# A two-block transformer kernel: square sums on TensorE, order of a turn, one more raw buffer, work behind the last turn

## The chip, the core and the metric

The kernel runs on one core of one Trainium2 chip. The metric is the device time of one execution in microseconds (us), the median of three runs. TensorE (PE in the rows; its weight loads are PEld) multiplies matrices, VectorE (DVE) and ScalarE (ACT) work element by element, GpSimd (POOL) does a few small things, and SyncE (SP) issues nearly all transfers (DMAs) from memory. Each engine executes its own instructions strictly in the order of the program; a wait of one instruction holds up all behind it on that engine.

## The reference, cut to what matters

Two transformer blocks follow each other over 256 tokens of width 2048. The change touches the first stage of the first block's first layer only, which computes this, for the tokens `x` and for a context `ctx` of 256 tokens:

```python
def _rmsnorm(x, w):
    xf = x.astype(jnp.float32)
    y = xf * lax.rsqrt(jnp.mean(xf * xf, axis=-1, keepdims=True) + EPS)
    return (y * w.astype(jnp.float32)).astype(x.dtype)
...
    shift, scale, gate = jnp.split(jax.nn.silu(c) @ w_mod + b_mod, 3, axis=-1)
    hx = _rmsnorm(x, norm_w) * (1 + scale[:, None]) + shift[:, None]
    a_h, a_b, a_c, a_z, q, k, v, r_z = _split_in(hx @ w_in)
```

So before the first large product `hx @ w_in` can begin, the mean square of each token is wanted, and shift and scale, which are products of one vector with two thirds of the 2048 x 6144 matrix `w_mod`.

## The kernel before, in words

All data is float32. The features lie on the 128 partitions: x and ctx are 16 tiles of 128 features x 256 tokens each (`qT`, `kT`, `v` and `big1` hold them at first, 512 KB per transfer). A main weight is split into a rounded part `whi` (ScalarE) and a rest `wlo` (VectorE), and each product is made of three multiplications on TensorE; all of them have line L370.

The first stage runs in eight turns j = 0 to 7 (`mod0_cols`), one for every 256 of the 2048 features. A turn reads eight blocks of `w_mod` of 512 KB in four steps g = 0 to 3 of two blocks each, and TensorE multiplies each step's blocks in eight instructions (L490) into one side bank of PSUM. After g = 3 ScalarE copies that bank to `macc0` (L494), TensorE transposes it (L502), VectorE adds the parts up and adds the bias (`mod0_turn`: mcol, L473, L510), and `make_hx` builds two tiles of hx as `a` tiles (VectorE L526, ScalarE L527, VectorE L528). These two tiles are then multiplied by their rows of the k columns and half of the q columns of `w_in` (512 KB and 256 KB per turn): 36 multiplications in six pieces of six, which the next turn weaves between its four steps: two pieces behind g = 0, one behind g = 1, two behind g = 2, one behind g = 3 (turn 1 has none behind g = 0). The other 256 q columns follow behind the stage, again in eight units of two tiles each.

Ahead of the turns, `squares` takes the squares of x and ctx on ScalarE (eight instructions, L436), sums them over the tiles on VectorE (L439, L441), and in turn 0, behind g = 1, TensorE sums over the partitions (`tok_sums`, L232). VectorE and GpSimd take the root (L218), and `bcast_rows` spreads the result over the partitions with TensorE (L243), behind g = 2.

The blocks land in raw buffers: of the two blocks of a step the first takes the pool `wraw` (4 buffers, which the `w_in` blocks of the turn use too), the second the pool `wst` (3 buffers). SyncE issues in program order, and an issue waits until the buffer's last reader is through. TensorE's order is the order of the code; the scheduler orders the other engines, with priorities (`hot` puts work forward). Beside the later units a background queue `modq` sums the remaining columns of `w_mod` on VectorE (L458, L461), from its own raw blocks, also in `wraw`.

Of the kernel before, what the change touches and what calls it, by code (L numbers as in the profile page):

```python
# [13 lines left out]
AF = mybir.ActivationFunctionType  # L14
# [5 lines left out]
P = 128  # L20
# [142 lines left out]
def kernel(ctx: ExitStack, tc: tile.TileContext, x, cx, vec, w_mod, w_in, ret_decay_f, ret_decay_b,  # L163
# [7 lines left out]
    def mk(pool, shape, tag, dt=F32, bufs=None):  # L171
        uid[0] += 1
        return pool.tile(shape, dt, tag=tag, name=f"{tag}_{uid[0]}", bufs=bufs)
# [234 lines left out]
    xr = [None] * KT  # L408
    cr_ = [None] * KT
    rb = [None, None]  # L410
    xin = []
    for s, src in enumerate((x, cx)):
        for a in range(2):
# [17 lines left out]

    def squares(s):

        for g in range(4):
            sq = mk(ap_, [P, 1024], f"a{14 + g % 2}")
            nc.scalar.activation(out=sq, in_=xin[2 * s + g // 2][:, 4 * (g % 2):4 * (g % 2) + 4, :]  # L436
                                 .rearrange("p k t -> p (k t)"), func=AF.Square)
            acc = mk(tb, [P, L], "tmp") if g else sqa[s]
            nc.vector.tensor_reduce(out=acc, in_=sq.rearrange("p (k t) -> p t k", k=4), axis=AX.X, op=ALU.add)  # L439
            if g:  # L440
                nc.vector.tensor_tensor(out=sqa[s], in0=sqa[s], in1=acc, op=ALU.add)  # L441


    modc = [[smalls[f"mod{l}{v}"] for v in range(2)] for l in range(2)]
# [34 lines left out]
    def mod0_cols(j, weave):  # L479


        pr = side_ps()
        for g in range(4):
            raws = []
            for a in range(2):
                raws.append(mk(wst if a else wraw, [P, 2, 512], "raw"))
                nc.sync.dma_start(out=raws[a], in_=w_mod[j, 2 * g + a])
            for q in range(4):
                k = 4 * g + q
                nc.tensor.matmul(pr[32 * q:32 * q + 32, :], lhsT=s2w[:, 2 * k:2 * k + 32], rhs=raws[q // 2][:, q % 2, :],  # L490
                                 start=g == 0, stop=g == 3, tile_position=(0, 32 * q))
            if g == 3:
                row = mk(t1, [P, 512], "macc0")
                nc.scalar.copy(out=row, in_=pr)  # L494
                rows[j] = row
            weave(j, g)

# [161 lines left out]
    def layer(l):  # L659
# [30 lines left out]
        def qkv(g):  # L690
            nonlocal at
            if l == 0 and g == 0:
# [1 line left out]
                b = Block(wl, [(col("k", 0), 512), (col("q", 0), 256)], mov, T, "fm", KT)  # L694
                b.ps = [[main_ps() for _ in range(4)], [main_ps(), side_ps()]]
                line = []
                rinv = []

                def more(n):
                    for _ in range(n if line else 0):  # L700
# [3 lines left out]
                            line.pop(0)  # L704

                def weave(j, g):
                    if j == 0:
                        if g == 1:
                            for s in range(2):
                                rinv.append(rsq(mean_eps(tok_sums([sqa[s]]), 2, D), 2, f"rq{s}"))  # L710
                        if g == 2:
                            for s in range(2):
                                rb[s] = bcast_rows(rinv[s], 2, f"rb{s}")
                    else:
                        more((2, 1, 2, 1)[g] if j > 1 else (0, 1, 2, 1)[g])
                    if g == 3:
                        mod0_turn(j)
                        for k in (2 * j, 2 * j + 1):
                            make_hx(l, k)
                        line.append([b.steps([2 * j, 2 * j + 1], True), 6])  # L720
                        next(line[-1][0])
                        if j == 5:
                            nc.sync.dma_start(out=cr, in_=kcr)

                for j in range(KT // 2):
                    mod0_cols(j, weave)
                while line:
                    more(1)
                kT, qT = mk(t1, [P, 4, 512], "kT"), mk(t1, [P, 4, T], "qT")
# [6 lines left out]
                pumps.append(dmaq)  # L736
                pri[0] = PRI
                layer_tables(l)
                evac(qT, Block(wl, [(col("q", 0) + 256, 256)], mov, T, "fm", KT).run(ks)[0], 2, 1.0, T)
                rope(qT)  # L740
                ps = run("v", g, 512, "tm")
                v = mk(t1, [P, 4, 512], "v")
# [566 lines left out]
```

## Time and profile before

| | |
|---|---|
| median of 3 runs | 2839.34 us (2837.23 to 2842.5) |
| the profiled execution, its own time | 2839.79 us |
| its span, first to last instruction | 2838.1 us |
| PE busy | 2795.9 us, 99% of the span |
| DVE, ACT, POOL busy | 1777.6, 1224.9, 85.5 us |
| mean DMA rate | 184 GB/s |
| mean granted TensorE clock | 0.997 |

In the rows further below, engines stand in the order PE, PEld, DVE, ACT, POOL where they have no name. The busy share of PE counts matmuls whose ends are modelled, so that a matmul which waits can look long. The chain of work that ended last, followed back from the end, is 95% PE over the whole span. The stage of the change is its first 150 us.

### The profile page before, as it was taken

What the parts mean: (1) busy time and instruction counts of PE and PEld (TensorE: products, weight loads), DVE (VectorE), ACT (ScalarE), POOL (GpSimd) and SP (SyncE); (2) the same over time, 40 slices, a digit from 0 to 9 for tenths busy, and PEclk for the clock granted to TensorE, in tenths of its full rate; (3) what the DMA queues carried; (4) which work ended last, traced back from release to release, by engine and by line L of the source; (5) the groups of instructions that cost most, each with busy time, mean ns of one, the idle gap of its engine ahead of it and who ended that gap; (6) DMA issues with size and microseconds to landing.
All of it is one profiled execution on the core that took longest, in us unless ns stands there. A gap on an engine that the chain in (4) does not pass through costs nothing.

```text
span 2838.1 us, 37511 instructions
## 1 busy us (share of the span) xinstructions
PE 2795.9 (99%) x14206; PEld 2348.8 (83%) x14206; DVE 1777.6 (63%) x2952; ACT 1224.9 (43%) x1960; POOL 85.5 (3%) x143
## 2 busy tenths in 40 slices
PE   6999999999999999999999999999999999999999
PEld 3588888888888878888888888888888888888878
DVE  5475765667686764754767766665766666654465
ACT  3333322332242253533556655554644544444464
POOL 0010000000000000000000010000000000000000
PEclk9999999999999999999999999999999999999999
DMA  9864454444465545655656665556556665666655
GB/s 339 315 186 134 141 157 155 149 137 156 149 206 172 171 141 163 226 156 175 216 177 216 197 201 168 167 170 189 163 190 191 188 192 187 191 193 193 208 172 169
DMA packets 159158, 522.80 MB, mean 184 GB/s; under 512 B 18232, under 2 KB 36928, under 8 KB 158720
## 3 DMA queue, kind: packets, MB, share of 16 engines
q1 hardware_dynamic: 155296, 508.78, 56.2%
q0 software_dynamic: 3392, 11.29, 1.3%
q8 instruction: 111, 1.82, 0.3%
q14 instruction: 71, 0.58, 0.1%
q10 hardware_dynamic: 288, 0.33, 0.0%
HBM read 509.83 MB, written 7.88 MB: 182 GB/s over the span
## 4 chain that ended last, share of the span: by engine, by line
PE 95%; DVE 2%; DMA 2%; ACT 1%; issue 0%; POOL 0%; SPq 0%; DVEq 0%; ACTq 0%; POOLq 0%
PE mm L370 88%; DMA raw<-in_w_mod_dram 1%; PE sd L490 1%; PE sd L612 1%; PE sd L599 1%; PE sd L606 0%; DVE wlo L317 0%; PE sd L370 0%; PE sd L590 0%; PE sd L467 0%; DVE tmp L439 0%; DMA raw<-in_w_in_dram 0%; DVE macc L461 0%; PE sd L1185 0%; ACT whi L316 0%
## 5 line engine op out<-in xcount | busy, mean ns | idle before, releaser
L317 DVE TENSOR_TENSOR wlo<-raw,whi 128x1024 fp32r<-128x1024 f32 (+1 forms) x764 | 917.2, 1201 | 767.0 <-ACT whi L316 756.6
L316 ACT CAST whi<-raw 128x1024 fp32r<-128x1024 f32 (+1 forms) x764 | 786.5, 1030 | 1313.7 <-PE mm L370 1117.2
L370 PE MATMUL mm<-a,whi 128*128 128x512 f32 x3552 | 1153.2, 394 | 3.3 <-ACT a L527 1.9
L370 PEld LDWEIGHTS mm<-a,whi 128*128 128x128 f32 x3552 | 661.4, 188 | 163.0 <-issue 18.4
L370 PE MATMUL mm<-a,wlo 128*128 128x512 f32 (+1 forms) x2288 | 781.7, 342 | 0.0
L370 PE MATMUL mm<-h,whi 128*128 128x512 f32 x1920 | 671.1, 392 | 0.1
L370 PE MATMUL mm<-h,wlo 128*128 128x256 f32 x1920 | 541.2, 282 | 0.0
L370 PEld LDWEIGHTS mm<-a,wlo 128*128 128x128 f32 x2288 | 430.8, 188 | 50.9 <-DVE wlo L317 0.2
L370 PEld LDWEIGHTS mm<-h,whi 128*128 128x128 f32 x1920 | 360.7, 188 | 75.7 <-issue 0.6
L370 PEld LDWEIGHTS mm<-h,wlo 128*128 128x128 f32 x1920 | 363.1, 189 | 0.0
L461 DVE SCALAR_TENSOR_TENSOR macc<-raw,s,macc 128x512 f32<-128x512 f32 x420 | 292.0, 747 | 82.6 <-DMA raw<-in_w_mod_dram 81.6
L370 PE MATMUL mm<-whi,f 128*128 128x512 f32 x704 | 217.0, 389 | 0.0
L370 PE MATMUL mm<-whi,h 128*128 128x512 f32 (+1 forms) x576 | 172.0, 373 | 0.0
L370 PE MATMUL mm<-whi,a 128*128 128x512 f32 x512 | 158.8, 389 | 0.0
L370 PEld LDWEIGHTS mm<-whi,f 128*128 128x128 f32 x704 | 132.1, 188 | 27.4
L370 PE MATMUL mm<-wlo,f 128*128 128x512 f32 x352 | 136.9, 389 | 0.0
L370 PEld LDWEIGHTS mm<-whi,h 128*128 128x128 f32 x576 | 104.3, 189 | 16.9
L370 PEld LDWEIGHTS mm<-whi,a 128*128 128x128 f32 x512 | 96.1, 188 | 20.0
L370 PE MATMUL mm<-wlo,h 128*128 128x512 f32 (+1 forms) x288 | 105.6, 366 | 0.0
L370 PE MATMUL mm<-wlo,a 128*128 128x512 f32 x256 | 99.6, 389 | 0.0
L370 PE MATMUL mm<-whi,o 128*128 128x512 f32 x256 | 80.1, 391 | 0.0
L370 PEld LDWEIGHTS mm<-wlo,f 128*128 128x128 f32 x352 | 66.1, 188 | 13.7
(277 smaller groups left out, 1967.2 us busy)
## 6 DMA issues: line engine op xcount, KB each, us to landing
raw<-in_w_in_dram SPq DMA_DIRECT2D x344, 512.0 KB, 3.7
raw<-in_w_mod_dram SPq DMA_DIRECT2D x192, 512.0 KB, 4.3
raw<-in_w_gate_up_dram SPq DMA_DIRECT2D x176, 512.0 KB, 3.5
raw<-in_w_out_dram SPq DMA_DIRECT2D x96, 512.0 KB, 3.6
raw<-in_w_down_dram SPq DMA_DIRECT2D x88, 512.0 KB, 3.5
raw<-in_w_pli_gate_dram SPq DMA_DIRECT2D x24, 512.0 KB, 4.2
raw<-in_w_in_dram SPq DMA_DIRECT2D x16, 256.0 KB, 5.4
raw<-in_w_pli_gate_dram SPq DMA_DIRECT2D x16, 256.0 KB, 3.3
```

The lines of the kernel that those rows point to most:

```text
L316: nc.scalar.copy(out=hi, in_=raw)
L317: nc.vector.tensor_tensor(out=lo, in0=raw, in1=hi, op=ALU.subtract)
L370: nc.tensor.matmul(o[b], lhsT=l_, rhs=r_, start=d0 + a == 0 and b == 0, stop=d0 + a == self.nk - 1 and b == len(tri) - 1)
L461: nc.vector.scalar_tensor_tensor(out=acc[v], in0=raw[:, a, :], scalar=sc, in1=acc[v], op0=ALU.mult, op1=ALU.add)
L490: nc.tensor.matmul(pr[32 * q:32 * q + 32, :], lhsT=s2w[:, 2 * k:2 * k + 32], rhs=raws[q // 2][:, q % 2, :], start=g == 0, stop=g == 3, til ...
L599: nc.tensor.matmul(ps[:, t * L:(t + 1) * L], lhsT=kT[:, q0 + t * P:q0 + (t + 1) * P], rhs=qT[:, q0:q0 + L], start=True, stop=True)
L612: nc.tensor.matmul(po[:, t * P:(t + 1) * P], lhsT=sc[:, jt * L + t * P:jt * L + (t + 1) * P], rhs=v[:, 2 * s + jt, :], start=(jt == 0), st ...
```

## The change

`squares` now sums on TensorE: behind each of the eight squares stand eight multiplications of a 128x128 tile of squares by a column of ones (`ones[:, 0:1]`), 64 in all, which accumulate in two main banks of PSUM per tensor; the mean, the root and the spreading follow, the spreading of x behind g = 1 and that of ctx behind g = 2 of turn 0. The reductions and additions on VectorE are gone. The second block of a turn's step g = 1 takes a buffer of the pool `big` (`big0`), and the pools of the other blocks are exchanged: the first block of each step takes `wst`, the second `wraw` (or `big0`). The `w_in` blocks of a turn are split, in the code, ahead of `mod0_turn` and `make_hx`, and these two and the copy to `macc0` get the high priority. Behind the last turn the first of the eight units of the remaining q columns (`q2`) is moved ahead of the last turn's own 36 multiplications, in two side banks.

```diff
@@ -408,6 +408,7 @@
+    rin = [None, None]
...
@@ -431,14 +432,19 @@
     def squares(s):
 
+        ps = [main_ps() for _ in range(2)]
         for g in range(4):
-            sq = mk(ap_, [P, 1024], f"a{14 + g % 2}")
-            nc.scalar.activation(out=sq, in_=xin[2 * s + g // 2][:, 4 * (g % 2):4 * (g % 2) + 4, :]
-                                 .rearrange("p k t -> p (k t)"), func=AF.Square)
-            acc = mk(tb, [P, L], "tmp") if g else sqa[s]
-            nc.vector.tensor_reduce(out=acc, in_=sq.rearrange("p (k t) -> p t k", k=4), axis=AX.X, op=ALU.add)
-            if g:
-                nc.vector.tensor_tensor(out=sqa[s], in0=sqa[s], in1=acc, op=ALU.add)
+            sq = mk(ap_, [P, 4, L], f"a{8 + 4 * s + g}")
+            nc.scalar.activation(out=sq, in_=xin[2 * s + g // 2][:, 4 * (g % 2):4 * (g % 2) + 4, :], func=AF.Square)
+            for k in range(4):
+                for t in range(2):
+                    nc.tensor.matmul(ps[t][:, 0:1], lhsT=sq[:, k, t * P:(t + 1) * P], rhs=ones[:, 0:1],
+                                     start=g + k == 0, stop=g + k == 6)
+        v = mk(sm, [P, 2], "mv")
+        for t in range(2):
+            nc.vector.tensor_scalar(out=v[:, t:t + 1], in0=ps[t][:, 0:1], scalar1=1.0 / D, scalar2=EPS, op0=ALU.mult,
+                                    op1=ALU.add)
+        rin[s] = rsq(v, 2, f"rq{s}")
...
@@ -483,7 +489,8 @@
             for a in range(2):
-                raws.append(mk(wst if a else wraw, [P, 2, 512], "raw"))
+                pool, tag = ((wst, "raw"), (wraw, "raw"), (big, "big0"))[(0, 1, 0, 2, 0, 1, 0, 1)[2 * g + a]]
+                raws.append(mk(pool, [P, 2, 512], tag))
                 nc.sync.dma_start(out=raws[a], in_=w_mod[j, 2 * g + a])
...
             if g == 3:
                 row = mk(t1, [P, 512], "macc0")
-                nc.scalar.copy(out=row, in_=pr)
+                with hot():
+                    nc.scalar.copy(out=row, in_=pr)
...
@@ -704,26 +711,26 @@
                 def weave(j, g):
-                    if j == 0:
-                        if g == 1:
-                            for s in range(2):
-                                rinv.append(rsq(mean_eps(tok_sums([sqa[s]]), 2, D), 2, f"rq{s}"))
-                        if g == 2:
-                            for s in range(2):
-                                rb[s] = bcast_rows(rinv[s], 2, f"rb{s}")
-                    else:
+                    if j == 0 and g in (1, 2):
+                        rb[g - 1] = bcast_rows(rin[g - 1], 2, f"rb{g - 1}")
+                    if j > 0:
                         more((2, 1, 2, 1)[g] if j > 1 else (0, 1, 2, 1)[g])
                     if g == 3:
-                        mod0_turn(j)
-                        for k in (2 * j, 2 * j + 1):
-                            make_hx(l, k)
                         line.append([b.steps([2 * j, 2 * j + 1], True), 6])
                         next(line[-1][0])
+                        with hot():
+                            mod0_turn(j)
+                            for k in (2 * j, 2 * j + 1):
+                                make_hx(l, k)
...
                 for j in range(KT // 2):
                     mod0_cols(j, weave)
+                more(2)
+                q2 = Block(wl, [(col("q", 0) + 256, 256)], mov, T, "fm", KT)
+                q2.ps = [[side_ps(), side_ps()]]
+                q2.run(ks[:2])
                 while line:
                     more(1)
...
-                evac(qT, Block(wl, [(col("q", 0) + 256, 256)], mov, T, "fm", KT).run(ks)[0], 2, 1.0, T)
+                evac(qT, q2.run(ks[2:])[0], 2, 1.0, T)
```

On TensorE, at the start of the program, stood these rows before (sd_175 is the bank of turn 0, raw its blocks, L232 the sums over partitions of the squares in sqa, L243 the spreading of x's roots):

```order
L490 MATMUL sd_175<-raw_176,s2w_129 32x512 x2
L490 MATMUL sd_175<-raw_178,s2w_129 32x512 x2
L490 MATMUL sd_175<-raw_184,s2w_129 32x512 x2
L490 MATMUL sd_175<-raw_186,s2w_129 32x512 x2
L232 MATMUL sd_192<-ca_83,sqa_2_84 128x1 x2
L232 MATMUL sd_199<-ca_83,sqa_3_85 128x1 x2
L490 MATMUL sd_175<-raw_206,s2w_129 32x512 x2
L490 MATMUL sd_175<-raw_208,s2w_129 32x512 x2
L243 MATMUL sd_214<-dg_215,ca_83 128x128
L243 MATMUL sd_214<-dg_218,ca_83 128x128
```

In their place stands now (mm_180 and mm_181 are the sums of ctx, a_37 its last tile of squares; these are the last two of 64 multiplications of that kind, and then turn 0 begins):

```order
L441 MATMUL mm_180<-ca_83,a_37_212 128x1
L441 MATMUL mm_181<-ca_83,a_37_212 128x1
L497 MATMUL sd_233<-raw_234,s2w_129 32x512 x2
L497 MATMUL sd_233<-raw_236,s2w_129 32x512 x2
L497 MATMUL sd_233<-raw_242,s2w_129 32x512 x2
L497 MATMUL sd_233<-big_50_244,s2w_129 32x512 x2
L243 MATMUL sd_250<-dg_251,ca_83 128x128
L243 MATMUL sd_250<-dg_254,ca_83 128x128
L497 MATMUL sd_233<-raw_259,s2w_129 32x512 x2
L497 MATMUL sd_233<-raw_261,s2w_129 32x512 x2
L243 MATMUL sd_267<-dg_268,ca_83 128x128
```

The sums moved from behind the fourth block of `w_mod` to ahead of the first, and are 64 multiplications in place of 8.

On SyncE, the issues of the last turn were these before, with what each waits for beside its lane (PE: TensorE is through with the buffer's last content; DVE: VectorE has split a `w_in` block; the last two rows are that turn's own `w_in` blocks):

```order
L487 DMA raw_959<-in_w_mod_dram 128x1024 [waits DMAHW3_49,PE_49]
L487 DMA raw_961<-in_w_mod_dram 128x1024 [waits DMAHW2_49]
L487 DMA raw_979<-in_w_mod_dram 128x1024 [waits DMAHW5_49,PE_49]
L487 DMA raw_981<-in_w_mod_dram 128x1024 [waits DMAHW4_49]
L487 DMA raw_993<-in_w_mod_dram 128x1024 [waits DMAHW7_49,DVE_49]
L487 DMA raw_995<-in_w_mod_dram 128x1024 [waits DMAHW6_49,PE_49]
L487 DMA raw_1013<-in_w_mod_dram 128x1024 [waits DMAHW0_49,DVE_49]
L487 DMA raw_1015<-in_w_mod_dram 128x1024 [waits DMAHW2_49,PE_49]
L341 DMA raw_1060<-in_w_in_dram 128x1024 [waits DMAHW1_49]
L341 DMA raw_1066<-in_w_in_dram 128x2x256 [waits DMAHW3_49,PE_49]
```

and are now:

```order
L494 DMA raw_1003<-in_w_mod_dram 128x1024 [waits DMAHW1_49,PE_49]
L494 DMA raw_1005<-in_w_mod_dram 128x1024 [waits DMAHW4_49,DMAHW2_49,PE_49]
L494 DMA raw_1023<-in_w_mod_dram 128x1024 [waits DMAHW3_49]
L494 DMA big_226_1025<-in_w_mod_dram 128x1024
L494 DMA raw_1037<-in_w_mod_dram 128x1024 [waits DMAHW5_49,PE_49]
L494 DMA raw_1039<-in_w_mod_dram 128x1024 [waits DMAHW6_49,PE_49]
L494 DMA raw_1057<-in_w_mod_dram 128x1024 [waits DMAHW7_49,DMAHW1_49,PE_49]
L494 DMA raw_1059<-in_w_mod_dram 128x1024 [waits DMAHW0_49,DVE_49]
L341 DMA raw_1073<-in_w_in_dram 128x1024 [waits DVE_49]
L341 DMA raw_1079<-in_w_in_dram 128x2x256 [waits DMAHW2_49,PE_49]
```

Of the eight `w_mod` issues the fifth and the seventh waited for a split (DVE) before, and now the eighth alone does.

On TensorE, behind the last turn's transposes, stood before (the first row is the last product of the turn before; mm_169 is the first of the last turn's 36 rows):

```order
L370 MATMUL sd_174<-a_217_937,wlo_225_955 128x512
L370 MATMUL mm_169<-a_238_1042,whi_245_1062 128x512 [waits Activation_49]
L370 MATMUL mm_169<-a_238_1042,whi_245_1062 128x512 [waits DVE_49]
L370 MATMUL mm_169<-a_238_1042,wlo_246_1063 128x512
L370 MATMUL mm_169<-a_241_1051,whi_245_1062 128x512 [waits Activation_49]
L370 MATMUL mm_169<-a_241_1051,whi_245_1062 128x512 [waits DVE_49]
L370 MATMUL mm_169<-a_241_1051,wlo_246_1063 128x512
```

and now, with sd_1128 and sd_1129 for the moved unit:

```order
L370 MATMUL sd_232<-a_219_993,wlo_213_968 128x512
L370 MATMUL sd_1128<-a_72_311,whi_249_1132 128x512 [waits Activation_49]
L370 MATMUL sd_1128<-a_72_311,whi_249_1132 128x512
L370 MATMUL sd_1128<-a_72_311,wlo_250_1133 128x512 [waits DVE_49]
L370 MATMUL sd_1128<-a_75_320,whi_249_1132 128x512 x2
L370 MATMUL sd_1128<-a_75_320,wlo_250_1133 128x512
L370 MATMUL sd_1129<-a_72_311,whi_249_1132 128x512 [waits PE_49]
L370 MATMUL sd_1129<-a_72_311,whi_249_1132 128x512
L370 MATMUL sd_1129<-a_72_311,wlo_250_1133 128x512
L370 MATMUL sd_1129<-a_75_320,whi_249_1132 128x512 x2
L370 MATMUL sd_1129<-a_75_320,wlo_250_1133 128x512
L370 MATMUL mm_227<-a_240_1098,whi_233_1075 128x512 [waits Activation_49]
```

Twelve multiplications (x2 counts two) moved into that gap, with a wait for VectorE's `wlo` at the third. On VectorE, a little later, the split for the unit behind it was ahead of the `dm` rows (wlo_264 here):

```order
L461 SCALAR_TENSOR_TENSOR macc_265_1200<-raw_1226,s_14_98,macc_265_1200 128x512 [waits DVE_49]
L461 SCALAR_TENSOR_TENSOR macc_266_1201<-raw_1226,s_14_98,macc_266_1201 128x512 [waits DVE_49]
L317 TENSOR_TENSOR wlo_264_1185<-raw_1182,whi_263_1184 128x2x256 [waits DMAHW6_49,PE_49,Activation_49]
L780 MEMSET big_331_1647 128x8
L781 MEMSET big_331_1647 128x8
L574 TENSOR_TENSOR dm_1684<-dm_1684 128x128 [waits Pool_49]
L574 TENSOR_TENSOR dm_1744<-dm_1744 128x128 [waits Pool_49]
```

and stands now behind them and behind two rows that wait for a block of the background queue:

```order
L582 TENSOR_TENSOR dm_1728<-dm_1728 128x128 [waits DMAHW5_49,Pool_49]
L582 TENSOR_TENSOR dm_1782<-dm_1782 128x128 [waits Pool_49]
L583 COPY dm_1728<-dm_1728 128x128 [waits DVE_49]
L583 COPY dm_1782<-dm_1782 128x128 [waits DVE_49]
L467 SCALAR_TENSOR_TENSOR macc_264_1262<-raw_1288,s_14_98,macc_264_1262 128x512 [waits DMAHW2_49]
L467 SCALAR_TENSOR_TENSOR macc_265_1263<-raw_1288,s_14_98,macc_265_1263 128x512
L317 TENSOR_TENSOR wlo_260_1229<-raw_1226,whi_259_1228 128x2x256 [waits DMAHW6_49,PE_49,Activation_49]
```

## Rows read from the trace of the kernel before

**Rows 1.** Windows of 20 us: busy us (count) per engine; clock, DMA share, GB/s.

```profile
100.00:120.00 20.00, 19.94 (x100) 10.90 (x97) 5.61 (x17) 4.67 (x9) 0.00 (x0) 1.00 0.99 373
...
160.00:180.00 20.00, 20.00 (x90) 16.53 (x90) 17.12 (x23) 5.99 (x8) 2.18 (x4) 1.00 0.83 255
```

**Rows 2.** Windows of 2 us, columns as in rows 1.

```profile
16.00:18.00 2.00, 1.54 (x6) 0.41 (x8) 2.00 (x2) 0.77 (x2) 0.00 (x0) 1.00 1.02 416
...
24.00:26.00 2.00, 1.46 (x8) 1.13 (x12) 0.93 (x6) 0.00 (x0) 0.86 (x2) 0.50 1.01 388
...
30.00:32.00 2.00, 1.30 (x8) 0.00 (x0) 0.00 (x0) 0.83 (x3) 0.00 (x0) 0.80 0.85 346
```

**Rows 3.** Timeline of weight loads: start, length, instruction, [idle before <-releaser].

```profile
16.43 0.22 PEld L490 LDWEIGHTS sd<-raw,s2w 128*32 128x32 f32 x4 [16.43 <-DVE sqa L441]
...
24.54 0.93 PEld L232 LDWEIGHTS sd<-ca,sqa 128*128 128x128 f32 x4 [2.69 <-DVE sqa L441]
...
34.81 0.14 PEld L490 LDWEIGHTS sd<-raw,s2w 128*32 128x32 f32 x4 [2.03 <-DMA raw<-in_w_mod_dram]
...
45.23 0.59 PEld L502 LDWEIGHTS sd<-ca,macc 128*128 128x128 f32 x4
```

**Rows 4.** Timeline of ACT: the copies behind turns 0, 1 and 7.

```profile
31.40 0.59 ACT L494 COPY macc<-sd 128x512 f32<-128x512 f32 x1 [1.17 <-PE sd L490]
...
44.18 0.59 ACT L494 COPY macc<-sd 128x512 f32<-128x512 f32 x1 [7.28 <-PE sd L490]
...
133.67 0.59 ACT L494 COPY macc<-sd 128x512 f32<-128x512 f32 x1 [6.90 <-PE sd L490]
```

**Rows 5.** Chain of work that ended last, one turn's length: start, length, what.

```profile
76.75 0.44 PE sd L502 x4
...
82.12 1.31 PE mm L370 x4
...
83.46 0.73 PE mm L370 x2
84.19 1.42 PE sd L490 x6
...
88.60 1.00 PE sd L490 x8
89.60 1.59 PE mm L370 x6
91.19 0.44 PE sd L502 x4
```

**Rows 6.** Timeline of ACT: the second of the eight squares.

```profile
7.17 1.06 ACT L436 ACTIVATE a<-qT 128x1024 f32<-128x1024 f32 x1 [0.18 <-DMA qT<-in_x_dram]
```

**Rows 7.** DMA issues of the first 150 us: KB each, median us to landing.

```profile
raw<-in_w_mod_dram SPq DMA_DIRECT2D x67, 512.0 KB, 5.7
```

**Rows 8.** Timeline of DVE behind the last turn.

```profile
135.70 1.22 DVE L317 TENSOR_TENSOR wlo<-raw,whi 128x1024 fp32r<-128x1024 f32 x1
...
139.05 0.69 DVE L317 TENSOR_TENSOR wlo<-raw,whi 128x512 fp32r<-128x512 f32 x1
...
141.92 0.48 DVE L528 SCALAR_TENSOR_TENSOR a<-tmp,mod,a 128x256 fp32r<-128x256 f32 x1
```

**Rows 9.** Timeline of PE there.

```profile
139.65 0.50 PE L370 MATMUL mm<-a,whi 128*128 128x512 f32 x1 [1.34 <-ACT a L527]
```

**Rows 10.** Chain of work that ended last, from the last turn on.

```profile
142.46 6.19 PE mm L370 x26
...
150.00 54.40 PE mm L370 x240
```

**Rows 11.** Timeline of POOL behind the last turn.

```profile
144.42 4.47 POOL L570 TENSOR_SCALAR_AFFINE_SELECT dm<-dm 128x128 f32<-128x128 f32 x1 [1.61 <-ACT dm L564]
```

**Rows 12.** Chain of work that ended last, at 509 us.

```profile
509.09 8.76 DMA raw<-in_w_mod_dram
```

**Rows 13.** Groups by line, first 150 us: count | busy us, mean ns.

```profile
L243 PE MATMUL sd<-dg,ca 128*128 128x128 f32 x8 | 2.4, 461 | 0.0
```

More of the change, by code (lines that the diff above doesn't have):

```diff
@@ L696, in qkv @@
                 line = []
-                rinv = []
                 def more(n):
```

## The prediction

> **What bounds the kernel now.** I read the windows first, to see where TensorE is not full. From 150 us on it is: between 160 and 180 us it is busy for 20.00 of 20 us [rows 1], and so it goes on to the end. Whatever the stage of the turns gives back therefore moves the end by as much. In the stage itself the transfers are near their limit: 100 to 120 us has a DMA share of 0.99 with 373 GB/s [rows 1], and 16 to 18 us reached 416 [rows 2].
>
> The timeline and the chain of waits then say what ends last in each part. TensorE has its first block at 16.43 us, and stands still for 2.69 us up to 24.54, behind VectorE, which sums squares [rows 3]; it cools to a granted clock of 0.50 and gets back only between 30 and 32 us [rows 2]. Turn 0 ends at 31.40 us, turn 1 at 44.18, turn 7 at 133.67 [rows 4]: the last six take 89.49 us, 14.92 each.
>
> One of them shows what a turn is made of [rows 5]. From its transposes at 76.75 to the next at 91.19 are 14.44 us. Two pieces in it are long: six multiplications end 2.07 us after their start (82.12 to 84.19) where six elsewhere take 1.59, and a step takes 1.42 where another takes 1.00. The second is a raw block that has not landed (0.42). The first (0.48) is hx: the fifth of these six starts at 83.46, 6.27 us behind the transposes (76.75 + 0.44), which is how long VectorE needs for the new tiles. Without either a turn is 13.54 us of TensorE; with hx alone late, 14.02.
>
> **Squares on TensorE.** Eight reductions and six additions leave VectorE. Nothing but TensorE waited for them, so they are worth TensorE's gap. In their place come 64 multiplications ahead of turn 0. I price them by the load of a 128x128 weight in float32: four take 0.93 us at the half clock and 0.59 later [rows 3], so 64 are 14.9 or 9.4 us. They start when the first square is there, about 7.2 us, when ScalarE takes up the second [rows 6], and lie in time in which TensorE has no block yet. They can't be through before about 17.4 us: a block of 524 KB at 416 GB/s [rows 2] is 1.26 us, so the last input lands 1.26 ahead of 16.43, and 15.2 + 1.06 for its square [rows 6] + 8 x 0.15 is 17.4. All at the half clock, they end at 22.1.
>
> Which clock? The window at 16 to 18 us prints 1.00 [rows 2], but four loads of a block take 0.22 us there and 0.14 at 34.81 [rows 3], so the first work of the program ran slow in spite of the print. After 24.5 us TensorE worked for some six us at 0.50 before the clock rose [rows 2]. I take six us slow, 26 multiplications, and 38 fast, 5.6 us: through at 18.8. The Trainium skill, "TensorE: Matmul & The Clock Gate", Part 1, says that the throttled state is the default and that activity ends it; the two lengths of a load agree, and the printed 1.00 does not. By the print all 64 would be fast and end at the 17.4 that the inputs allow, which changes the sum by less than 0.5 us.
>
> Turn 0 then goes at the pace of its blocks: eight at 1.26 us from 16.43 on land by 25.3, the last step is 1.0, the end 26.4. The seventh block takes the first one's buffer and is issued once TensorE has used the first step, at 18.8 + 1.0; with a landing of 5.7 us in the median [rows 7] that is some half a us behind its place among the blocks. I take 26.9 for the end of turn 0, against 31.40: **-4.5 us** (bounds: -5.0, and -0.4 with all squares slow).
>
> Turn 1 has its first blocks called for early, but its last one waits for the buffer that turn 0's first split frees: 12.8 us before, 13.2 now, **+0.4**.
>
> **One more buffer, pools exchanged.** What counts is how long before its use a block is issued. From steps of 1.0 and pieces of 1.5 to 1.6 [rows 5] I place step g = 2 at 6.7 us into a turn and g = 3 at 10.8. Before, the fifth block of a turn waited for a split, which starts right behind the transposes and takes 1.22 [rows 8]: it was issued at about 15.0 and used at 13.5 + 6.7 = 20.2, 5.2 later, less than the 5.7 to land [rows 7], and the sixth stood behind it on SyncE's queue; the first pair had 5.8 and 5.3. Now the tightest is the second block with 5.8, while its neighbour was called 2.6 earlier, and all others have 8 or more. So the waits for blocks should go, and what is late next is hx. VectorE's rows within a turn stand in the same order as before, since the earlier split in the code and the higher priority change nothing there; these two edits I cost at nothing. If they did move hx, the 0.48 that it costs a turn bounds them. Six turns of 14.02 are 84.1 us against 89.49: -5.4. The transfers must keep up: a turn's 4.98 MB at 373 GB/s [rows 1] is 13.4 us, under 14.02 but near, so I leave 0.5 us of waits: **-4.9** (bounds: 13.54 a turn, -8.2; no better than before, 0).
>
> **The unit behind the last turn.** After the transposes TensorE has 12 multiplications left, then idles for 1.34 us to 139.65 and after, and is in its flow at 142.46 [rows 9, 10]. The moved unit is 12 multiplications; at 6.19 us for 26 [rows 10] that is 2.86. It fills the gap but for one wait: its third needs the `wlo` that VectorE has at 139.74 [rows 8], so it ends at about 142.1, when the last hx tile, begun at 141.92 [rows 8], is not yet wanted. The last turn's 36 then end at about 150.3 of the old count, where before the twelve still followed from 150.00 on [rows 10]: -2.5. Something comes back. The split of the next unit now stands on VectorE behind the `dm` rows, which wait for GpSimd until 148.89 [rows 11], and behind two additions that wait for a background block. Its buffer becomes free in two moves: the moved unit is split by 139.74, the block that follows in that buffer lands and is split by about 145, and only then is the background block issued, 4 to 5 us to land, since little else is under way. That is 149.5; with two additions and the split 151.5, where TensorE wants it at 150.8: 0.7 back. **-1.8** (bounds: -2.5, +2.6).
>
> **The sum.** -4.5 + 0.4 - 4.9 - 1.8 = -10.8 us. The profiled execution took 2839.79 with a span of 2838.1, 0.45 above the median of the three runs, so the same difference goes on the median: 2839.34 - 10.8 = **2828.5 us**.
>
> **Rivals.**
> *The squares stay at the half clock.* They are almost all weight loads with one column of work behind each, and no row shows what such a stretch does to the clock; the slow first loads speak for it, the rise after six us of mixed work [rows 2] against. Turn 0's first step then waits for 22.1, the seventh block is issued at 23.1, the eighth lands at 30, turn 0 ends at 31: -0.4 + 0.4 - 4.9 - 1.8 = -6.7, 2832.6.
> *The buffer gives nothing.* The blocks wait for the transfers' rate: 0.99 at 373 GB/s speaks for it, the 416 against. The six turns stay at 14.92: -5.9, 2833.4.
> *The tail stalls.* A background block once held the chain for 8.76 us [rows 12], 4.4 more than I count, and TensorE would wait that long in the second unit: -10.8 + 4.4 = -6.4, 2832.9.
> *hx is in time as well.* Turns are 13.54: 3.3 less, 2825.
> *Slower.* One mechanism: a multiplication of squares costs like one of the spreading, 0.461 us [rows 13]. 64 are 29.5, through at 36.7; the seventh block is issued at 37.7, the eighth lands at 44.7, turn 0 ends at 45.8: +14.4. Turn 1 then has its data and gains about 2: +14.4 - 2 - 4.9 - 1.8 = +5.7, 2845. It decides from 0.37 us each on; four loads in 0.93 speak against it.
>
> **How the numbers follow.** Forecast 0.50, hx in time 0.10, half clock 0.15, buffer 0.12, tail 0.08, slower 0.05. Runs of this kernel differ by some 2.6 us around the median, and 0.2% is 5.7 us, about what a measurement can tell from no change: faster ends at 2833.7. The three rivals near 2833 fall on its fast side in six or seven of ten cases, so faster is 0.50 + 0.10 + 0.10 + 0.08 + 0.05 = 0.83, slower 0.04, the rest 0.13. The range goes from 2820 (2825, with the earliest turn 0, no 0.7 at the tail, no 0.5 of waits, and the scatter) to 2836 (the three rivals with the scatter). The forecast's own is 2824 to 2832.
>
> **What would show it.** Right: no gap on TensorE between 19 and 25 us, weight loads of 0.15 us from about 14 us on, copies to `macc0` at about 27, 40 and 124 us, in each turn six multiplications of 2.1 us but steps of 1.0, and TensorE full from the last transposes on but for two waits of some 1 us. Wrong: squares with loads of 0.23 us to their end, a first copy after 30, steps of 1.4 as before, or a wait of some us in the second moved unit, with a background block as its releaser.

## The result: 22 us slower, and the profile after

The changed kernel takes 2862.78 us in the median of four runs (2859.44 to 2864.13), where the kernel before, run beside it, takes 2840.53 (2837.23 to 2842.5): a ratio of 1.008 with a 95% interval of 1.0067 to 1.0092. The profiled execution took 2864.13 us with a span of 2862.4, against 2838.1, so 24.3 us are to be found in its trace.

The first loss is at the start. The timeline of TensorE, and below it of its weight loads and of SyncE's queue (start, length, instruction, [idle before <-releaser]); the last row is from the list of SyncE's waits of the first 60 us (us in total, times, longest):

```profile
7.62 27.44 PE L441 MATMUL mm<-ca,a 128*128 128x1 f32 x128 [7.62 <-DMA ca<-in_k_a_dram]
34.99 2.77 PE L497 MATMUL sd<-raw,s2w 128*32 128x512 f32 x10
```

```profile
7.59 27.38 PEld L441 LDWEIGHTS mm<-ca,a 128*128 128x128 f32 x128 [7.59 <-ACT a L438]
...
38.56 0.87 PEld L243 LDWEIGHTS sd<-dg,ca 128*128 128x128 f32 x4 [1.66 <-issue]
...
40.55 0.52 PEld L243 LDWEIGHTS sd<-dg,ca 128*128 128x128 f32 x4 [0.84 <-DVE dg L242]
```

```profile
11.26 26.49 SPq L494 DMA_DIRECT2D raw<-in_w_mod_dram  x4
```

```profile
SPq L494 <- PE sd L497: 28.8, 8, 20.6
```

The 64 multiplications of squares leave 128 records, 0.214 us each, through at 35.0 us; ScalarE had its last square at 16.1. The first block is multiplied at 34.99 where before it was at 16.43 [rows 3], and SyncE waits 20.6 us for TensorE to be through with the first buffer: of the four issues in its row two go out by 12.9 us, and the next only at 36.95. Four loads take 0.87 us behind this stretch and 0.52 two microseconds later: TensorE came out of 27 us of squares at its lower clock.

The copies behind turns 0, 1 and 7, which answer to [rows 4], on ScalarE, and then one event on GpSimd behind the tail of the stage, of before and of after:

```profile
42.99 0.58 ACT L502 COPY macc<-sd 128x512 f32<-128x512 f32 x1 [1.32 <-PE sd L497]
...
57.12 0.59 ACT L502 COPY macc<-sd 128x512 f32<-128x512 f32 x1 [8.62 <-PE sd L497]
...
142.01 0.59 ACT L502 COPY macc<-sd 128x512 f32<-128x512 f32 x1 [6.37 <-PE sd L497]
```

```profile
254.38 0.70 POOL L218 TENSOR_TENSOR rr<-ve,ca 128x2 f32<-128x2 f32 x1 [6.90 <-DVE ve L631]
```

```profile
260.65 0.70 POOL L218 TENSOR_TENSOR rr<-ve,ca 128x2 f32<-128x2 f32 x1 [4.66 <-DVE ve L639]
```

| stretch | before | after | change | forecast |
|---|---|---|---|---|
| to the end of turn 0 | 31.40 | 42.99 | +11.6 | -4.5 |
| turn 1 | 12.78 | 14.13 | +1.4 | +0.4 |
| turns 2 to 7 | 89.49 | 84.89 | -4.6 | -4.9 |
| from there to the event on GpSimd | 120.71 | 118.64 | -2.1 | -1.8 |
| from there to the end of the span | 2583.7 | 2601.7 | +18.0 | 0 |

So at 260 us the kernel is 6.3 us late, and 18 us more are lost where the diff changes no line. The waits of TensorE between 150 and 1420 us, largest total first (engine, line <- releaser: us in total, times, longest), of before and of after:

```profile
PE sd L599 <- DVE qT L688: 2.2, 1, 2.2
PE sd L243 <- DVE dg L242: 1.4, 2, 0.8
PE mm L370 <- DVE a L528: 0.5, 1, 0.5
PE mm L370 <- DVE b L376: 0.3, 1, 0.3
```

```profile
PE mm L370 <- DVE b L376: 3.0, 2, 2.6
PE mm L370 <- DVE b L815: 2.0, 1, 2.0
PE mm L370 <- DVE big L795: 2.0, 1, 2.0
PE sd L243 <- DVE dg L242: 1.6, 2, 0.8
PE mm L370 <- ACT tmp L835: 1.4, 1, 1.4
PE sd L607 <- DVE qT L696: 1.2, 1, 1.2
PE mm L370 <- DVE wlo L317: 1.0, 1, 1.0
PE mm L370 <- ACT a L535: 0.8, 1, 0.8
PE mm L370 <- DVE a L536: 0.8, 2, 0.6
PE mm L370 <- DVE big L376: 0.7, 1, 0.7
```

4.4 us of waiting have become 14.5, in new places, mostly for VectorE. The one at 382 us shows the kind. VectorE's timeline, TensorE's, and windows of 2 us (columns as in [rows 1]):

```profile
376.79 4.06 DVE L467 SCALAR_TENSOR_TENSOR macc<-raw,s,macc 128x512 f32<-128x512 f32 x6
380.76 1.22 DVE L317 TENSOR_TENSOR wlo<-raw,whi 128x1024 fp32r<-128x1024 f32 x1
381.90 0.42 DVE L815 TENSOR_TENSOR a<-mm,a 128x256 f32<-128x256 f32 x1
382.23 0.41 DVE L815 TENSOR_TENSOR b<-mm,b 128x256 f32<-128x256 f32 x1
```

```profile
380.37 0.39 PE L370 MATMUL mm<-a,wlo 128*128 128x512 f32 x1
382.80 0.70 PE L370 MATMUL mm<-a,whi 128*128 128x512 f32 x2 [2.04 <-DVE b L815]
...
384.42 1.05 PE L370 MATMUL mm<-a,whi 128*128 128x512 f32 x2
```

```profile
382.00:384.00 2.00, 1.20 (x5) 1.05 (x6) 2.00 (x7) 1.65 (x5) 0.00 (x0) 1.00 1.00 295
384.00:386.00 2.00, 2.00 (x6) 1.58 (x5) 2.00 (x7) 1.02 (x4) 0.00 (x0) 0.52 0.52 213
386.00:388.00 2.00, 2.00 (x7) 1.53 (x7) 1.97 (x4) 0.15 (x1) 0.00 (x0) 0.63 0.00 0
```

TensorE is through with a block and wants its banks of PSUM back. VectorE, which has to read them out (L815), first sums a background column (`macc`, six rows), and a split stands between. TensorE stands 2.04 us, and then its clock falls to 0.52: two multiplications take 1.05 us instead of 0.62 for some 3 us more. From 383.57 to 387.91 four groups take 4.34 us where four at the full clock take 2.74: 1.6 us on top of the wait. The clock falls like this four times between 260 and 1420 us (0.83 in the 10 us from 380, 0.88 and then 0.95 from 670, 0.83 from 1050 and from 1220), and once in the kernel before (0.83 in the 10 us from 520). An estimate from these windows is 1.7 us for each fall: at most some 5 of the 18 us go with the clock, 10.1 are waits, and the other 3 are not placed.

### The profile page after: what moved, and what is told of

Same layout as the page of the kernel before. It is cut to its first block, busy times and chain, and to the rows that moved or that the text cites. A ratio compares the mean times of both kernels' runs of the same rounds, so it can differ in the third digit from the quotient of the medians.

```text
span 2862.4 us, 37727 instructions
## 1 busy us (share of the span) xinstructions
PE 2824.4 (99%) x14326; PEld 2376.0 (83%) x14326; DVE 1759.2 (61%) x2940; ACT 1224.9 (43%) x1960; POOL 81.6 (3%) x143
## 4 chain that ended last, share of the span: by engine, by line
PE 50%; DVE 0%; issue 0%; POOL 0%; ACT 0%; POOLq 0%; ACTq 0%
PE mm L370 48%; PE sd L1192 0%; PE sd L1198 0%; POOL rq L218 0%; PE sd L1262 0%; PE sd L1092 0%; PE sd L1057 0%; PE sd L1073 0%; PE sd L1046 0%; PE sd L1110 0%; ACT whi L316 0%; PE sd L243 0%; PE sd L232 0%; PE sd L1085 0%; PE sd L1086 0%
## 5 line engine op out<-in xcount | busy, mean ns | idle before, releaser
L370 PE MATMUL mm<-a,whi 128*128 128x512 f32 x3488 | 1140.9, 396 | 11.0 <-DVE b L376 3.0
L370 PEld LDWEIGHTS mm<-a,whi 128*128 128x128 f32 x3488 | 651.8, 189 | 172.7 <-issue 22.5
L370 PE MATMUL mm<-a,wlo 128*128 128x512 f32 (+1 forms) x2256 | 771.8, 342 | 1.0 <-DVE wlo L317 1.0
```

Of the source, the lines that this page charges most:

```text
L370: nc.tensor.matmul(o[b], lhsT=l_, rhs=r_, start=d0 + a == 0 and b == 0, stop=d0 + a == self.nk - 1 and b == len(tri) - 1)
```

## The experiments

**First run: the background queue one step on.** `modq` advances once per unit that is pumped, on two of three pumps. The units of `q2` are eight, all behind the line that hangs the queue in; the change moves one of them ahead of that line, so seven pump it. SyncE's order shows it (`in_w_in` blocks are units, `in_w_mod` blocks the background; from the transfers of `lg` on), of before and of the changed kernel:

```
L537 DMA lg_254_1144<-in_ret_decay_b_dram 128x8
L341 DMA raw_1164<-in_w_in_dram 128x2x256
L341 DMA raw_1182<-in_w_in_dram 128x2x256
L453 DMA raw_1202<-in_w_mod_dram 128x1024
L341 DMA raw_1208<-in_w_in_dram 128x2x256
```

```
L545 DMA lg_255_1208<-in_ret_decay_b_dram 128x8
L341 DMA raw_1226<-in_w_in_dram 128x2x256
L341 DMA raw_1244<-in_w_in_dram 128x2x256
L459 DMA raw_1264<-in_w_mod_dram 128x1024
L341 DMA raw_1270<-in_w_in_dram 128x2x256
```

They read alike, but the first unit behind `lg` is number 1 of eight before and number 2 after: every background block stands one unit later. The edit:

```diff
                 pumps.append(modq)
+                modq.step()
                 pumps.append(dmaq)
```

> The changed kernel with one more step of the background queue, taken at the point where the queue is hung in, so that its rows stand again in the same place among the units as before the change. Own theory: the waits of TensorE at 381, 533, 676, 815, 1052 and 1219 us come from background rows of VectorE that stand one unit later and so meet the evacuations at the ends of blocks; with the step they go, and some 16 of the 17 us lost behind 360 us come back: 2862.8 - 16 = 2846.5 us (2844 to 2849). First copy to macc0 unchanged at 43.0 us. Rival: the waits come from the moved unit or from the shift of the whole program by 6 us against the transfers: the time stays at 2861 to 2864.

Measured: 2848.28 us (2847.55 to 2850.91), ratio to before 1.0036 (1.0023 to 1.0048), 14.5 us less than the changed kernel. First copy at 42.90. The waits of TensorE between 150 and 1420 us, and VectorE's rows at the place of the wait at 382 us:

```profile
PE sd L607 <- DVE qT L696: 3.4, 1, 3.4
PE sd L243 <- DVE dg L242: 1.7, 2, 0.9
PE mm L370 <- DVE b L376: 0.3, 1, 0.3
PE mm L370 <- DVE wlo L317: 0.2, 1, 0.2
```

```profile
371.35 4.05 DVE L467 SCALAR_TENSOR_TENSOR macc<-raw,s,macc 128x512 f32<-128x512 f32 x6
375.32 1.22 DVE L317 TENSOR_TENSOR wlo<-raw,whi 128x1024 fp32r<-128x1024 f32 x1
376.46 0.41 DVE L816 TENSOR_TENSOR a<-mm,a 128x256 f32<-128x256 f32 x1
```

The same column now ends 5.4 us earlier, while TensorE stands where it stood: its row at 380.37 us is in both traces, with no wait behind it here. The waits are those of before in kind and nearly in sum (5.6), and the rival falls: neither the multiplications of the moved unit nor the shift of the program makes them. Nor does `dmaq`, the other queue that the moved unit no longer pumps: it stays one step late in this run. One wait that was there before has grown (`qT`, 2.2 to 3.4 us), which may be most of the 1.8 us by which the run lies over its forecast.

**Second run: squares as before the change, all else as changed.** The functions `squares` and `weave` of before, in the changed kernel:

```diff
-        ps = [main_ps() for _ in range(2)]
...
+            nc.vector.tensor_reduce(out=acc, in_=sq.rearrange("p (k t) -> p t k", k=4), axis=AX.X, op=ALU.add)
```

> The changed kernel with the square sums back on VectorE (reductions, additions, sums and spreading as before the change), all else as changed, the late background rows included. Own theory: the first turn ends at 31.4 us again and the second at about 44.5, turns 3 to 8 keep their 14.0 us, the tail its gain of 2 us, and the 17 us behind 360 us stay lost, since squares have nothing to do with them: 2839.8 + 0.4 - 4.6 - 2.0 + 17 = 2850.6 us (2847 to 2854). Rival: the late start of the first turns is the cause of everything that is lost later as well: 2839.8 - 6.2 = 2833.6.

Measured: 2848.83 us (2847.24 to 2852.24), ratio 1.0039 (1.0026 to 1.0053). Copies at 31.54 and 129.41, waits between 150 and 1420 us 15.7 in sum. The squares cost 14 us, and the later waits stand without them: those aren't theirs.

**Third run: ones as the weight, squares as moving columns.**

```diff
-                for t in range(2):
-                    nc.tensor.matmul(ps[t][:, 0:1], lhsT=sq[:, k, t * P:(t + 1) * P], rhs=ones[:, 0:1],
+                nc.tensor.matmul(ps[:, :L], lhsT=oner, rhs=sq[:, k, :], start=g + k == 0, stop=g + k == 6)
...
-        rin[s] = rsq(v, 2, f"rq{s}")
+        nc.gpsimd.tensor_tensor(out=rb[s], in0=v, in1=C("nhalf")[:, 0:1].broadcast_to([P, L]), op=ALU.pow)
```

> The changed kernel with the extra background step, and with the squares summed the other way around: a block of ones is the weight, the squares (written in the rounded format of the main products, which changes their low bits) go through as 32 moving blocks of 256 columns, and the sums come out spread over all partitions, so that the four spreading multiplications go. Own theory: it is the price of a weight load per column of result that made the changed form dear; here TensorE is through about 1 us behind the last square, at 17.5 us (at the half clock, 0.40 us each, 20.5 at the latest); turn 0 ends at 27 to 29.5, total 2839.8 - 4.5 + 0.4 - 4.6 - 2.0 = 2829 us (2827 to 2833). Rival: the first turn is bound by its transfers whatever the squares cost, and ends at 31.4: 2833.6 or more.

Measured: 2906.13 us, ratio 1.0237 (1.0223 to 1.0251), a miss by 77 us, and by my own addition. Besides the exchange, this run has the squares in the rounded format of the main products, and the step of the first run. GpSimd's timeline, the weight loads, and the first copy:

```profile
13.28 41.14 POOL L447 TENSOR_TENSOR rb<-tmp,ca 128x256 f32<-128x256 f32 x1 [12.77 <-DVE tmp L445]
```

```profile
8.85 3.67 PEld L443 LDWEIGHTS mm<-a,dg 128*128 128x128 f32 x16 [8.85 <-ACT a L441]
12.67 0.54 PEld L443 LDWEIGHTS mm<-a,dg 128*128 128x128 f32 x4
```

```profile
26.77 0.59 ACT L502 COPY macc<-sd 128x512 f32<-128x512 f32 x1 [10.30 <-PE sd L497]
```

The power of 256 columns takes GpSimd 41.1 us per stream (of two columns 0.7), and hx waits for it. But what the run was for it shows: 32 records, 0.23 us per load at first and 0.14 from 12.7 us on, TensorE through 0.8 us behind the last square, and the first copy at 26.8, where the prediction had wanted it.

**Fourth run: the changed form in one pass.** Squares and ones in the rounded format (with the step of the first run):

```diff
+            sq = mk(ap_, [P, 4, L], f"a{8 + 4 * s + g}", F32R)
+                    nc.tensor.matmul(ps[t][:, 0:2], lhsT=sq[:, k, t * P:(t + 1) * P], rhs=one,
```

> The changed kernel with the extra background step, squares in the changed form (squares as weights, ones as moving columns, two columns of which one is used), but in the rounded format of the main products, which changes the low bits of the squares. Own theory: 128 records for 64 multiplications come from the full-precision format, which loads each weight twice; here there are 64, at the half clock's 0.214 us each 13.7 us: through at 21.3 us, first turn's end at about 30, total 2846.5 - 12 = 2834.5 us (2832 to 2837). Rival one, the clock rises within such a stretch if it is let go on: 0.14 us each, through at 17.5, total 2830. Rival two, the doubling is not of the format: 128 records, through at 35, total 2846.5.

Measured: 2833.97 us (2831.61 to 2837.29), ratio 0.9982 (0.9973 to 0.999); the first copy at 30.64. The weight loads:

```profile
8.81 13.73 PEld L443 LDWEIGHTS mm<-a,a 128*128 128x128 f32 x64 [8.81 <-ACT a L440]
```

64 records of 0.215: the doubling is that of the full-precision format, and the loads got no faster in these 14 us either. Both rivals fall.

**Fifth run: the wide form, mended.** The summed block is turned by two transposes, so that the power is again one of two columns (with the step):

```diff
+        pt = main_ps()
+        for t in range(2):
+            nc.tensor.transpose(pt[:, t * P:(t + 1) * P], u[:, t * P:(t + 1) * P], ident)
...
+        nc.vector.tensor_copy(out=v, in_=pt[:, :L].rearrange("p (t e) -> p t e", t=2)[:, :, 0])
+        rin[s] = rsq(v, 2, f"rq{s}")
```

> The wide squares of the third run, again with the rounded format and the extra background step, but the power no longer taken by GpSimd over 256 columns, which took 41.1 us for each stream there: the summed row block is turned by two transposes, the power is taken of two columns, and the spreading is as in the changed kernel. Own theory: all else in that run was as forecast (first copy to macc0 at 26.8 us), so here the first turn ends at 27 to 28 us, 3 us ahead of the one-pass form's 30.6, the turns keep 14 us, the last one ends near 125.5: 2834.0 - 3 = 2831 us (2828 to 2834). Rival: turn 1 waits for its blocks whatever turn 0 does, the last copy stays at 128: 2834.

Measured: 2827.45 us (2827.29 to 2829.46), ratio 0.996 (0.9945 to 0.9976): the fastest here, 12 us under before, with squares summed in the rounded format. TensorE's timeline and the first copy:

```profile
17.95 0.44 PE L448 MATMUL mm<-ca,tmp 128*128 128x128 f32 x2 [0.79 <-DVE tmp L445]
18.32 1.91 PE L501 MATMUL sd<-raw,s2w 128*32 128x512 f32 x12
...
24.65 1.98 PE L501 MATMUL sd<-raw,s2w 128*32 128x512 f32 x8
```

```profile
26.68 0.59 ACT L506 COPY macc<-sd 128x512 f32<-128x512 f32 x1 [1.55 <-PE sd L501]
```

Turn 1 takes 14.7 us (next copy at 41.34), so 0.8 of the 4.0 us that turn 0 gains over the fourth run is waited away there; the last copy comes at 125.17, 3.2 us earlier. The other 3.3 us between the two medians are placed in part: the profiled executions, whose spans differ by 5.8, show a fall of the clock in the fourth run behind 1020 us (0.83 in the 10 us from there), where the fifth stands at 1.00, and a longer one behind 2720 us (0.77 and 0.89 in 20 us, where the fifth has 0.83 in 10). That is some 3 us; whether the other executions differ in this way no trace shows.

**Sixth run: the buffers alone**, in the kernel before:

```diff
-                raws.append(mk(wst if a else wraw, [P, 2, 512], "raw"))
+                pool, tag = ((wst, "raw"), (wraw, "raw"), (big, "big0"))[(0, 1, 0, 2, 0, 1, 0, 1)[2 * g + a]]
+                raws.append(mk(pool, [P, 2, 512], tag))
```

> The kernel before with nothing but the three pools for the raw blocks. Own theory: turns 3 to 8 take 14.0 us each here too, first turn's end stays at 31.4: 2839.1 - 4.6 = 2834.5 us (2832 to 2837). Rival: the shorter turns need the other edits (copy and hx at high priority): then 14.9 a turn and 2839.

Measured: 2837.01 us (2832.61 to 2838.47), ratio 0.9989 (0.998 to 0.9998). The turns take 14.0 us each (copies 59.46 to 129.32), so the priorities aren't needed for that, as the prediction had it; the last copy is 4.35 us earlier than before, and in the profiled run 2.5 of them are gone by 252 us. Windows of 5 us behind the last turn:

```profile
134.00:139.00 5.00, 2.86 (x6) 1.55 (x7) 5.00 (x21) 3.53 (x9) 0.58 (x2) 0.76 0.76 264
139.00:144.00 5.00, 5.00 (x14) 3.86 (x14) 4.80 (x11) 2.68 (x7) 3.52 (x2) 0.56 0.18 52
```

The gap is the same as before the change (2.1 us of TensorE's waits here, 2.3 there), but here the clock fell after it, and there not:

```profile
138.00:143.00 5.00, 2.60 (x8) 1.16 (x7) 5.00 (x18) 3.48 (x9) 0.58 (x2) 1.00 0.75 256
143.00:148.00 5.00, 5.00 (x23) 4.13 (x22) 5.00 (x13) 4.41 (x11) 3.58 (x1) 1.00 0.19 56
```

**Seventh run: the moved unit alone**, in the kernel before, without the step:

```diff
+                more(2)
+                q2 = Block(wl, [(col("q", 0) + 256, 256)], mov, T, "fm", KT)
+                q2.ps = [[side_ps(), side_ps()]]
+                q2.run(ks[:2])
```

> The kernel before with nothing but the moved unit, without the extra background step. Own theory: -2 us at the tail, +17 us behind 360 us, since the background rows are one unit late here as well: 2839.1 + 15 = 2854 us (2850 to 2857), with waits of TensorE near 370, 660, 800 and 1200 us. Rival: the lateness only hurts with the other edits: 2837.

Measured: 2853.2 us (2851.35 to 2855.01), ratio 1.0047 (1.0033 to 1.0061), and 14.8 us of waits between 150 and 1420 us. Behind the event on GpSimd (251.51 us here) the profiled run takes 14.6 us more than before, where the changed kernel takes 18.0; between 260 and 1420 us its clock falls twice, against four times there. So the one moved unit makes all of the later waits and most of the later loss by itself, and the rival falls.

**Eighth run: squares as before, with the step** (the edits of the first two runs together).

> The second run (squares as before the change, all else as changed) with the extra background step. Own theory: both losses are gone and the two gains stay: 2848.8 - 15.5 = 2833.3 us (2831 to 2836). Rival: the step helps only where the first turns are late: 2848.

Measured: 2832.72 us (2829.98 to 2834.49), ratio 0.9974 (0.9965 to 0.9984), waits 5.1. The step is worth 16 us here, 14.5 in the changed kernel.

**Ninth run: the squares alone**, in the kernel before (`squares` and `weave` as changed).

> The kernel before with nothing but the changed square sums. Own theory: the first turn ends near 43 us as in the changed kernel, the second takes 1.3 us more than before, turns 3 to 8 keep the 14.9 us of before, nothing is lost behind 360 us: 2839.8 + 11.6 + 1.3 = 2852.7 us (2850 to 2855). Rival: while TensorE sums squares the blocks of the next turn land, and the later turns give part of it back: 2846.

Measured: 2849.28 us (2849.02 to 2854.3), ratio 1.0043 (1.0028 to 1.0058): 10 us over before, half way between the two. The profiled run is the longest of the four, with copies at 42.52, 59.19 and 148.28: 14.6 us late at the last turn, no less than forecast. Its clock fell once behind the last turn as well (0.80 in the 10 us from 150, 0.86 from 160), which is worth 3.4 us. Whether the other three runs, 5 us shorter, were spared that or gave something back elsewhere stays open. Together the three parts measured alone are 10.2 - 2.8 + 13.4 = 20.8 us, near the 22 of the change.

**Tenth run: TensorE warmed ahead of the squares** (with the step):

```diff
+    wp = side_ps()
+    for i in range(12):
+        nc.tensor.matmul(wp, lhsT=wr[:, :P], rhs=wr, start=i == 0, stop=i == 11)
     squares(0)
```

> The first run (changed kernel with the extra background step) with 12 multiplications of 512 columns on constants ahead of the squares, whose result nobody reads, so that TensorE comes to the squares at the full clock. It tells the two parts of the mis-sized price apart, number of records and clock. Own theory: one column behind each weight load doesn't hold the clock: records start near 0.1 us each and fall back to 0.214 after some us; through at 30 to 34 us, first copy at 38 to 42, total 2844 to 2848 us. Rival: the clock stays up: 128 records of 0.09 to 0.11 us, no later than the last square plus a few us, through at 20 to 23, first copy at 29 to 31, total 2834 to 2837.

Measured: 2842.9 us (2839.56 to 2847.72), ratio 1.0014 (1.0004 to 1.0023), first copy at 39.98. The weight loads, and windows of 4 us:

```profile
7.66 24.28 PEld L441 LDWEIGHTS mm<-ca,a 128*128 128x128 f32 x128 [0.86 <-ACT a L438]
```

```profile
8.00:12.00 4.00, 4.00 (x35) 4.00 (x35) 0.00 (x0) 3.39 (x4) 0.00 (x0) 0.94 1.03 420
12.00:16.00 4.00, 4.00 (x20) 4.00 (x20) 0.00 (x0) 3.33 (x4) 0.00 (x0) 0.50 1.02 417
```

35 loads in the first 4 us, 0.114 each, then 20 in 4 us with the clock printed at 0.50, and so on to the end: under the squares the clock fell, and it did not come back before they were through. A window of the changed kernel has the same 20 loads in 4 us under a printed 1.00:

```profile
24.00:28.00 4.00, 4.00 (x20) 4.00 (x20) 0.00 (x0) 0.00 (x0) 0.00 (x0) 1.00 0.00 0
```

The total is 5.4 us under the first run where the first copy is 2.9 earlier; 2.5 of that I can't place, and the spans of the two profiled executions differ by 1.7 only.

**Eleventh run: two steps** instead of one in the fifth run's kernel.

> The fifth run (wide squares, one extra background step) with two extra steps, so that the background rows stand one unit earlier than in the kernel before. Theory A: the place in the kernel before is a good one, not the start of a slope; one unit earlier the rows meet other ends of blocks, with waits of TensorE of 1 to 3 us at each: 2832 to 2845 us. Theory B: earlier is never worse, since lateness is what hurts: 2825 to 2829.

Measured: 2830.87 us (2828.22 to 2833.88), ratio 0.9972 (0.9961 to 0.9984). It lies between the two theories, and the spread of its runs overlaps the fifth run's. The waits of theory A do not appear: they are 5.3 us in sum, the longest 1.0, against 4.4 in sum in the fifth run. One unit later costs 15 us; one unit earlier costs 3.4 between the medians, which with this overlap is not sure.

## Why the prediction was wrong

**The price of the squares** failed, in two parts. "Four take 0.93 us at the half clock" were four records, and two records are one multiplication in full float32. The rows on record had it: the spreading, four multiplications in the program, stands there as x8 [rows 13]. (So do the "eight instructions" of a step in L490: the program has four.) And "I take six us slow, 26 multiplications, and 38 fast" held the clock's rise of [rows 2], which came in a stretch of mixed work, with blocks of 512 columns and the spreading, to be good for any work; 27 us of loads with one column each did not raise it, and in the tenth run it fell under them. Count and clock together took the price from the 11.6 us of the forecast to 128 x 0.214 = 27.4 us; with the full clock, and the count as it was, it would have been 128 x 0.114 = 14.6, and with half the count, and the clock as it was, 64 x 0.214 = 13.7. The slower rival had this right, at 0.43 us for a multiplication against its 0.461 and past its point of decision at 0.37: its 45.8 for the end of turn 0 was 43.0, and its 2845 is near the first run's 2848. That is in part luck: 0.461 is the mean length of a record in [rows 13], and records overlap there (eight in 2.4 us, so 0.6 for a multiplication); and the 2 us that it gave back in turn 1 were 1.4 more. The half-clock rival had the clock right and the count wrong; the fourth run is that rival made true, with 30.6 for its 31 and 2834.0 for its 2832.6. The Trainium skill, "FP8 and Floating Point Precision", TensorE Precision Notes, says that true FP32 goes through the array in four passes; the trace shows two weight loads per multiplication, and one in the rounded format. The Trainium skill, "TensorE: Matmul & The Clock Gate", Part 1, has the throttled state as the default that activity ends: the slow start agrees, an end by squares of this form no run shows.

**"Whatever the stage of the turns gives back therefore moves the end by as much"** failed by 18 us, the larger part. The windows at 160 us showed TensorE full, and that was true of the order that stood then. What I did not count was what the moved unit does besides its 12 multiplications: it pumps the background queue. I costed the move by TensorE's and VectorE's rows next to it and let the rest of the program pass unchanged, while one pump fewer moved every background row by a unit for more than 1000 us. The first, second, seventh and eighth runs show cause and size from both sides. At the ends of blocks VectorE had no room: waits of up to 2.6 us stood there, and behind some of them the half clock. With the order mended the sentence holds nearly: in the first run the time behind the event on GpSimd (at 260.70 us) is 2.2 us longer than before.

**What held.** Six turns at 14.02: 13.97 to 14.15 on average in the kernels with the new buffers (the excess in the changed one is its turn 2, with 15.0), the edits of priority at nothing. The tail at -1.8: -2.1, with waits of 0.53 and 0.21 us where 0.7 was allowed, though for the moved unit's own split and not behind the `dm` rows. The way from squares to the end of turn 0: 26.9 forecast, 26.7 and 26.8 as soon as the squares were through in time. The sum, 2828.5, lies 1 us from the fifth run, in which both losses are mended, and that nearness is in part luck. Turn 1 was too short in it: 13.2 forecast, 14.1 in the changed kernel and 14.7 in the fifth run; there 0.8 us more than forecast from turns 2 to 7 and 2.7 from the time behind the event on GpSimd (at 244.60 us), forecast at nothing, more than make up for it.

## What to carry to other kernels

When a unit of work is moved past the place where a queue is hung in, count what it pumps, and compare the order of every engine to the end of the program, not only around the move: a queue one step late is a new phase for all that follows. When a row is used as a price, count how many records one instruction leaves, and check that the clock under which the price was measured is the clock that the new work will have. A sum over partitions was cheap here with ones as the weight and the data as moving columns, 32 multiplications in the rounded format; in full float32 no run has that form.

## What the runs showed of the hardware that was not expected

A granted clock printed at the start of an execution was no evidence here: 1.00 stood over 27 us of loads at 0.214 us, 20 in 4 us, and in the tenth run 20 in 4 us stood under a printed 0.50. GpSimd's power took 0.16 us per column, 41.1 us for 256. Waits of TensorE of about 2 us were followed by the half clock in some executions and not in others: the gap behind the last turn cost nothing more in the kernel before and some 2.5 us in the sixth run's profile.
